# Operand formation, accumulated weight loads and small transposes in the seven-product FFN of a two-layer decoder trunk

## Chip, cores and metric

The kernel runs on one core of a Trainium2 chip. The metric is the device time of one execution in microseconds (us); where several runs are shown, their median counts. Engines are named as in the profile: PE is TensorE, DVE VectorE, ACT ScalarE, POOL GpSimd, SP SyncE.

## The reference, cut to what is computed

Two decoder layers on x of 512 tokens by 1024, all in float32. Each layer is a half-step SwiGLU FFN, a token mixer (layer 0: block-sparse attention, layer 1: pooling) and a second half-step FFN, each followed by a residual LayerNorm:

```python
def swiglu(x, w_gu, w_down):
    g, u = jnp.split(x @ w_gu, 2, axis=-1)        # 1024 -> 2 x 2816
    return (jax.nn.silu(g) * u) @ w_down          # 2816 -> 1024

for i in range(2):
    x = layer_norm(ALPHA * x + 0.5 * swiglu(x, ffn_w_gu[i, 0], ffn_w_down[i, 0]), ...)
    x = layer_norm(ALPHA * x + mixer_i(x), ...)
    x = layer_norm(ALPHA * x + 0.5 * swiglu(x, ffn_w_gu[i, 1], ffn_w_down[i, 1]), ...)
```

## The kernel before

**Passes.** Six phases follow each other: pass 0 FFN, 1 attention, 2 and 3 FFN, 4 pooling, 5 FFN (line 1009). Every float32 operand is split into a high half, copied by ACT (line 100), and the rest, which DVE subtracts (line 101); a product of two operands is then three matmuls (`mm3`, lines 103 to 107): high by low, high by high, low by high. The low half of the stationary operand is so wanted last, by line 107.

**Seven products.** A 2 x 2 block product is made with seven products of blocks in place of eight. The operands are sums and differences of the blocks: for weights in `Quad` (lines 132 to 148), for hidden activations in `Seven.seven` (lines 334 to 353). A product is known by its number 1 to 7; the order is 1, 2, 6, 5, 7, 3, 4 (`LATER`).

**Pieces and units.** A piece is 512 KB of weights, loaded by SP into a slot (line 215). The piece `s1` holds a21 + a22 and `s3` holds a21 + a11: SP loads a21, and once that has landed POOL issues a second, accumulating DMA that adds the other quarter (line 217). A unit is what one product needs of the weights, split into two halves in two more slots (`prepare`, line 227). Product 2 takes a12; product 6 takes a sum that DVE makes in place, a11 + s1, and also forms a12 + a11 + s1 for product 3 (`sums`, line 143); product 5 takes s1. Pieces are loaded in the order of the list `pieces`; down weights and attention's V weights come in two quads at once, whose pieces `two_quads` (line 166) interleaves as a11, a11, a12, a12, s1, s1, s3, s3, a22, a22. Units are split up to five ahead of the product that PE has finished (`PARTS`; `retire`, line 260, calls `run_ahead`).

**An FFN pass.** Quads 0 to 10 of gate and up columns give 256 hidden features each. Features 0 to 2047 go through the down projection in two groups of seven products (`down_product`, line 648), the rest through a plain product at the end. The first down group is placed inside quad 7 (`MIDDLE`): its product 1 comes ahead of the quad's product 4, the others behind it. The first group's hidden blocks are complete after quad 3. Its operands are made step by step by the generator `operands`: each `next(operands)` goes to the next `yield`. Before, steps stand behind (6, 7), (7, 7) and (3, 7), where (i, jj) is product i of quad jj, and behind the first five down products, there after `retire(2)`; four stand in the last quad for the second group. Operand 6 is made from `u2`, which uses the one buffer `ca` that the gate sums of each quad use too (line 692). Hidden operands 1 and 2 take two buffers of nine, of which the pass's own x takes seven; operand 6 takes the buffer that operand 1 leaves, operand 5 that of operand 2.

**Order.** PE's instructions run in the order of the text. Those of the other engines are put in order at build time by a planner: it keeps dependencies, prefers what stands earlier in the text, and by its own estimate of times fills an engine's free time with later work that is ready. On the chip each engine then works through its list in order, and waits where an input is not there. `tc.issue_after(ins)` keeps the instructions of its block that run on the engine of `ins` behind `ins`.

**Small inputs.** Pass 0 loads LayerNorm rows, a scale and the bias table's inputs at (1, 2) (`small_loads`, line 542). At (1, 6) `columns` (line 275) transposes the rows on PE into bank 6, from which DVE copies them (line 278), and `bias_rows` (line 553) then runs two matmuls into the same bank.

Of the kernel before, what the change touches and what calls it, by code (L numbers as in the profile page):

```python
# [28 lines left out]
ALU = mybir.AluOpType  # L29
# [30 lines left out]
MIDDLE = 7  # L60
# [23 lines left out]
def trunk(ctx, tc, x_in, xt, rel_bias, ln_g, ln_b, w_gu, w_dq, w_down, w_v, a_in, a_out, b_in, b_group, b_scale, b_out, onehot, out):  # L84
    nc = tc.nc
# [9 lines left out]
    def bank(i, name):  # L95
        return ps.tile([P, 512], F32, tag=f"b{i}", name=name)
# [6 lines left out]
    def mm3(acc, sh, sl, mh, ml, first, last, shared=False):  # L103

        nc.tensor.matmul(acc, sh, ml, start=first, stop=False, skip_group_check=shared)  # L105
        nc.tensor.matmul(acc, sh, mh, start=False, stop=False, skip_group_check=shared)  # L106
        nc.tensor.matmul(acc, sl, mh, start=False, stop=last, skip_group_check=shared)  # L107
# [8 lines left out]
    pieces, units, loaded = [], [], []  # L116
# [35 lines left out]
    QUADS = range(1, FF // 256)  # L152
# [12 lines left out]

    def two_quads(w, i):
        both = [Quad(w[i + q]) for q in range(2)]
        pieces[-10:] = [q.pieces[k] for k in range(5) for q in both]
        return both

    def ffn_units(l, m):
# [16 lines left out]
    for hp in range(H // 2):  # L188
        for part in (0, 1):
            a_plain(a_in[0], part * D + hp * 256)  # L190
        if hp == 0:
            both = two_quads(w_v, 0)
# [53 lines left out]
    def run_ahead(most=99):  # L246
        load_ahead()
        while len(parts) < min(len(units), taken[0] + most, retired[0] + PARTS + max(0, free() - 2) // 2 + early[0] + sum(i >= retired[0] for i in guests)):
            prepare()
            load_ahead()  # L250

    def weights():
        taken[0] += 1
        while len(parts) < taken[0]:
            while not all(p in loaded for p in units[len(parts)][1]):
                load()
            prepare()
        return parts[taken[0] - 1]

    def retire(count=1):  # L260

        retired[0] += count
        run_ahead()
# [11 lines left out]
    def columns(small):  # L275
        ct = bank(6, "cols_t")
        nc.tensor.transpose(ct[:, 0:2 * NL + NK], small[0:2 * NL + NK, GW + H:], ident[0:2 * NL + NK, 0:2 * NL + NK])
        nc.vector.tensor_copy(cols, ct[:, 0:2 * NL + NK])
# [24 lines left out]
    class Seven(Plain):  # L303
# [30 lines left out]
        def seven(self, b11, b21, b12, b22, room):  # L334

            self.take(1, b11)
            yield
            self.take(2, b21)
            yield
            nc.vector.tensor_tensor(b11, b11, b12, op=ALU.subtract)  # L340
            u2 = room()
            nc.vector.scalar_tensor_tensor(u2, b11, -1.0, b22, op0=ALU.mult, op1=ALU.subtract)
            yield
            self.take(6, u2)
            yield
            self.take(5, b11)
            yield
            self.form(7, b12, b12, -1.0, b22, ALU.add)
            yield
            self.take(3, b22)  # L350
            yield
            self.form(4, b21, u2, -1.0, b21, ALU.subtract)
            yield
# [188 lines left out]
    def small_loads():  # L542
        small = wp.tile([P, GW + H + P], F32, tag="slot", bufs=SLOTS, name="small")
        gs = wp.tile([H, GW], F32, tag="slot", bufs=SLOTS, name="gs")
        rows = small[:, GW + H:]
        nc.gpsimd.dma_start(rows[0:NL, :], ln_g.rearrange("l i (k p) -> (l i k) p", p=P))
        nc.gpsimd.dma_start(rows[NL:2 * NL, :], ln_b.rearrange("l i (k p) -> (l i k) p", p=P))
        nc.gpsimd.dma_start(rows[2 * NL:2 * NL + NK, :], b_scale[0].rearrange("(k p) -> k p", p=P))
        nc.gpsimd.dma_start(small[0:BUCKETS, 0:GW], onehot)
        nc.gpsimd.dma_start(small[0:BUCKETS, GW:GW + H], rel_bias)  # L550
        return small, gs
# [13 lines left out]

    BANKS = {1: 0, 6: 0, 7: 0, 4: 0, 2: 1, 5: 2, 3: 2}

    def ffn(n, x, dest):  # L570
        with tc.tile_pool(name=f"ffn{n}", bufs=1) as fp:
# [18 lines left out]
            def keep(i, jj, acc, bufs):  # L590
                kept[i, jj] = fp.tile([P, 512], F32, tag=f"kept{BANKS[i]}", bufs=bufs, name=f"kept{n}_{jj}_{i}")
                nc.scalar.activation(kept[i, jj], acc, AF.Copy)  # L592
# [43 lines left out]
            hid = [Seven(f"h{n}_{g}") for g in range(BLOCK // GROUP)]  # L636
# [11 lines left out]
            def down_product(i, g):  # L648


                if i in (1, 2, 5):
                    b0 = {1: (2, 6), 2: (0, 2), 5: (4, 4)}[i][g]
                    accs[g, BANKS[i]] = [bank(b0 + t, f"d{n}_{g}_{i}_{t}") for t in range(2)]
                acc = accs[g, BANKS[i]]
                for q in range(2):
                    wh, wl = weights()
                    for k in range(2):
                        c = slice(k * 512, (k + 1) * 512)
                        for t in range(2):
                            o = hid[g].parts[i][:, :, 2 * q + k, t * P:(t + 1) * P]  # L660
                            mm3(acc[t], o[:, 0], o[:, 1], wh[:, c], wl[:, c], q == 0 and k == 0 and i in (1, 2, 5),
                                q == 1 and k == 1 and i in (2, 3, 4), True)
                for t0, d, sign in {1: ((0, 0, 1),), 2: ((0, 0, 1),), 6: ((2, 0, 1),), 5: ((2, 1, -1),), 7: ((2, 1, -1),),
                                    3: ((2, 0, 1),), 4: ((0, 1, -1),)}[i]:
                    for t in range(2):
                        r = ax[:, t0 + t, d * 512:(d + 1) * 512]
                        nc.vector.scalar_tensor_tensor(r, acc[t], 0.5 / ALPHA * sign, r, op0=ALU.mult, op1=ALU.add)  # L667
                retire(2)
                if i in ((1, 2, 6, 5, 7) if g == 0 else (1, 2, 6, 5)):
                    next(operands)  # L670

            quads = {}
            for i, jj in ORDER:
                if jj >= FF:
                    down_product(i, jj - FF)
                    continue
                if n == 0 and (i, jj) == (1, 2):
                    with tc.issue_after(queued["acc"].ins):
                        onehots = small_loads()
                if n == 0 and (i, jj) == (1, 6):  # L680
                    columns(onehots[0])
                    bias_rows(*onehots)
                if n == 0 and i == 1 and 3 <= jj < 3 + NT:
                    with tc.issue_after(queued["load"].ins):
                        nc.sync.dma_start(ax[:, jj - 3, :], x_in[0, (jj - 3) * P:(jj - 2) * P, :])
                if (i, jj) == (1, 2):
                    load_residual()
                if i == 1:
                    quads[jj] = [bank(b, f"gu{n}_{jj}_{b}") for b in (2 * ((jj + 1) % 3), 2 * ((jj + 1) % 3) + 1)]
                if i == 2:  # L690
                    room(jj)
                    ca = fp.tile([P, 2, S], F32, tag="ca", name=f"ca{n}_{jj}")
                    cb = fp.tile([P, 2, 256], F32, tag="cb", name=f"cb{n}_{jj}")
                    quads[jj].append(bank(6 + jj % 2, f"gu{n}_{jj}_{6 + jj % 2}"))
                acc = quads[jj][BANKS[i]]
                for _ in product([acc[:, 0:256], acc[:, 256:512]], weights(), x.parts[i], i in (1, 2, 5), i in (2, 3, 4)):
                    pass
                if i in (1, 6):
                    keep(i, jj, acc, 2)
                elif i == 5:  # L700
                    keep(i, jj, acc, 1)
                elif i == 2:
                    add(ca[:, :, 0:256], acc, 1, jj)
                elif i == 3:
                    add(ca[:, :, 256:512], acc, 6, jj)
                    ins = gate(2 * jj, 0, 512, ca[:, 0, :], ca[:, 1, :], 1.0)
                    if 3 <= jj < 3 + NT:
                        update_residual(ins)
                elif i == 7:
                    add(cb, acc, 5, jj)  # L710
                    gate(2 * jj + 1, 256, 512, cb[:, 0, :], cb[:, 1, :], -1.0)
                else:
                    gate(2 * jj + 1, 0, 256, acc[:, 0:256], acc[:, 256:512], -1.0)
                retire()
                if jj == MIDDLE and i in (6, 7, 3) or jj == QUADS[-1] and i in (2, 6, 7, 3):
                    next(operands)

            pairs = {}
# [17 lines left out]
    def attention(n, x, dest):  # L736
        held[0] = 4
        with tc.tile_pool(name="att", bufs=1) as ap:
# [31 lines left out]
            def v_product(i):  # L770
                if i in (1, 2, 5):
                    accs[BANKS[i]] = [bank({1: 0, 2: 2, 5: 2}[i] + t, f"v{i}_{t}") for t in range(2)]
                acc = accs[BANKS[i]]
                for q in range(2):
# [285 lines left out]
```

## Time and profile before

| | |
|---|---|
| runs, us | 1695.34, 1691.97, 1692.09; median 1692.09 |
| profiled execution | 1694.32 us, of which span 1692.5 us |
| mean granted TensorE clock | 0.998 |
| PE busy | 1671.5 us, 99% |
| DVE busy | 1353.7 us, 80% |
| ACT busy | 865.8 us, 51% |
| POOL busy | 129.6 us, 8% |
| HBM read | 279.06 MB |

The span runs from the first to the last instruction of the profiled execution; the run's own time is 1.8 us longer. A busy share is an average over the whole span, and matmuls overlap, so the waits and the timelines of a stretch say more than the shares.

### The profile page before, as it was taken

The numbers are of one execution on the slowest core, as the hardware profiler recorded it, in microseconds if no ns is written. First come the engines' busy times: TensorE is split into PE (matmuls) and PEld (weight loads), VectorE is DVE, ScalarE is ACT, GpSimd is POOL, SyncE is SP. The second block draws the span as 40 slices with busy tenths as digits, with TensorE's granted clock in tenths as the row PEclk, the third lists the DMA queues.
The fourth block names the chain that finished last, engine by engine and source line by source line (L and its number), as shares of the span: only waits on it lengthen the run. The fifth ranks groups of instructions, "written<-read, shape, count | busy, mean of one in ns | idle before, by whom it ended". The sixth has DMA issues, their size and how long they took to land. (4 is left out here: it accounts for less than half of the span.)

```text
span 1692.5 us, 27752 instructions
## 1 busy us (share of the span) xinstructions
PE 1671.5 (99%) x11235; PEld 1547.8 (91%) x11235; DVE 1353.7 (80%) x1780; ACT 865.8 (51%) x1203; POOL 129.6 (8%) x172
## 2 busy tenths in 40 slices
PE   9999999999999999999999999999999999999998
PEld 9999899898888999979989999899898899998986
DVE  8686988798676878788788787897887887879697
ACT  6554555466444645545555555455454555445460
POOL 1102000000000001100000011000000101111000
PEclk9999999999999999999999999999999999999999
DMA  9778757805256177776683677866624647867541
GB/s 314 189 210 256 192 146 178 237 2 186 58 154 181 44 199 200 188 199 150 162 236 76 176 199 190 220 151 157 216 76 111 175 124 179 220 164 211 152 139 72
DMA packets 88848, 282.98 MB, mean 167 GB/s; under 512 B 8912, under 2 KB 22264, under 8 KB 88720
## 3 DMA queue, kind: packets, MB, share of 16 engines
q1 hardware_dynamic: 68304, 207.12, 36.9%
q0 software_dynamic: 20416, 74.09, 24.4%
q8 instruction: 88, 1.44, 0.3%
q14 instruction: 40, 0.33, 0.1%
HBM read 279.06 MB, written 4.74 MB: 168 GB/s over the span
## 5 line engine op out<-in xcount | busy, mean ns | idle before, releaser
L100 ACT ACTIVATE hi<-raw 128x1024 fp32r<-128x1024 f32 (+1 forms) x475 | 496.5, 1054 | 415.5 <-DVE lo L101 142.1
L101 DVE TENSOR_TENSOR lo<-raw,hi 128x1024 fp32r<-128x1024 f32 (+1 forms) x475 | 575.4, 1219 | 147.7 <-ACT hi L100 137.4
L105 PE MATMUL gu<-x,hi 128*128 128x256 f32 x2344 | 663.7, 283 | 1.6 <-DVE cb L595 0.9
L107 PE MATMUL gu<-x,lo 128*128 128x256 f32 x2344 | 663.6, 283 | 1.0 <-DVE lo L101 1.0
L106 PE MATMUL gu<-x,hi 128*128 128x256 f32 x2344 | 663.3, 283 | 0.0
L105 PEld LDWEIGHTS gu<-x,hi 128*128 128x128 f32 x2344 | 449.9, 192 | 3.7 <-DVE cb L595 1.3
L107 PEld LDWEIGHTS gu<-x,lo 128*128 128x128 f32 x2344 | 449.9, 192 | 1.6 <-DVE lo L101 1.6
L106 PEld LDWEIGHTS gu<-x,hi 128*128 128x128 f32 x2344 | 449.9, 192 | 0.4
L107 PE MATMUL d<-hi,xh 128*128 128x512 f32 x448 | 175.1, 391 | 7.1 <-DVE xh L101 7.1
L105 PE MATMUL d<-lo,xh 128*128 128x512 f32 x448 | 175.0, 391 | 0.2
L106 PE MATMUL d<-hi,xh 128*128 128x512 f32 x448 | 174.5, 389 | 0.0
L143 DVE TENSOR_TENSOR raw<-raw,raw 128x1024 f32<-128x1024 f32 x116 | 141.8, 1222 | 37.0 <-DMA raw<-in_ffn_w_dq 35.1
L217 POOL DMA_DIRECT2D raw<-in_ffn_w_gu x80 | 69.6, 870 | 797.3 <-DMA raw<-in_ffn_w_gu 325.2
L107 PEld LDWEIGHTS d<-hi,xh 128*128 128x128 f32 x448 | 84.1, 188 | 27.4 <-DVE xh L101 10.0
L105 PEld LDWEIGHTS d<-lo,xh 128*128 128x128 f32 x448 | 84.1, 188 | 18.1 <-DVE ca L595 0.6
L106 PEld LDWEIGHTS d<-hi,xh 128*128 128x128 f32 x448 | 84.1, 188 | 17.0
L592 ACT ACTIVATE kept<-gu 128x512 f32<-128x512 f32 x120 | 70.4, 587 | 48.4 <-PE gu L107 48.4
L105 PE MATMUL acc<-lo,h 128*128 128x512 f32 x192 | 75.2, 392 | 0.0
L107 PE MATMUL acc<-hi,h 128*128 128x512 f32 x192 | 74.7, 389 | 0.0
L106 PE MATMUL acc<-hi,h 128*128 128x512 f32 x192 | 74.7, 389 | 0.0
L101 DVE TENSOR_TENSOR x<-st,x 128x512 fp32r<-128x512 f32 (+1 forms) x65 | 56.0, 877 | 22.8 <-ACT x L100 22.5
L667 DVE SCALAR_TENSOR_TENSOR ax<-d,ax 128x512 f32<-128x512 f32 x112 | 72.5, 682 | 0.0
(176 smaller groups left out, 2234.6 us busy)
## 6 DMA issues: line engine op xcount, KB each, us to landing
raw<-in_ffn_w_gu SPq DMA_DIRECT2D x215, 512.0 KB, 4.9
raw<-in_ffn_w_gu POOLq DMA_DIRECT2D x80, 512.0 KB, 6.7
raw<-in_ffn_w_dq SPq DMA_DIRECT2D x80, 512.0 KB, 4.6
raw<-in_ffn_w_dq POOLq DMA_DIRECT2D x32, 512.0 KB, 7.7
raw<-in_ffn_w_down SPq DMA_DIRECT2D x24, 512.0 KB, 4.3
ax<-in_ln_b POOLq DMA_DIRECT2D x20, 512.0 KB, 8.0
raw<-in_a_w_in SPq DMA_DIRECT2D x16, 512.0 KB, 4.9
raw<-in_a_w_v SPq DMA_DIRECT2D x10, 512.0 KB, 4.5
```

The source lines that it names most:

```text
L100: nc.scalar.activation(hi, src, AF.Copy)
L101: return nc.vector.tensor_tensor(lo, src, hi.bitcast(F32), op=ALU.subtract)
L105: nc.tensor.matmul(acc, sh, ml, start=first, stop=False, skip_group_check=shared)
L106: nc.tensor.matmul(acc, sh, mh, start=False, stop=False, skip_group_check=shared)
L107: nc.tensor.matmul(acc, sl, mh, start=False, stop=last, skip_group_check=shared)
L143: nc.vector.tensor_tensor(d, d, more, op=ALU.add)
L217: queued["acc"] = nc.gpsimd.dma_start(p.tile, p.plus, accum_op=ALU.add)
L592: nc.scalar.activation(kept[i, jj], acc, AF.Copy)
L667: nc.vector.scalar_tensor_tensor(r, acc[t], 0.5 / ALPHA * sign, r, op0=ALU.mult, op1=ALU.add)
```

## The change

Five edits. (1) `two_quads` puts the s1 pieces in front of a12. (2) In `seven`, `b11 - b12` moves into the second step, and `b22 - b12`, until now formed with operand 7, gets a step of its own behind it; a group has nine steps instead of eight. (3) A list TAKES says behind which products a step is taken: four for the first group, at (6, 5), (6, 6), (3, 6) and (3, 7), and five in quad 10 for the second. (4) In `down_product` the step of an operand comes ahead of `retire(2)`, and in the first group's second product DVE's part of that `retire(2)` is held behind the operand just made. (5) `columns` moves from (1, 6) to (1, 4).

```diff
     def two_quads(w, i):
         both = [Quad(w[i + q]) for q in range(2)]
-        pieces[-10:] = [q.pieces[k] for k in range(5) for q in both]
+        pieces[-10:] = [q.pieces[k] for k in (0, 2, 1, 3, 4) for q in both]
...
             self.take(2, b21)
+            nc.vector.tensor_tensor(b11, b11, b12, op=ALU.subtract)
             yield
-            nc.vector.tensor_tensor(b11, b11, b12, op=ALU.subtract)
+            nc.vector.scalar_tensor_tensor(b12, b12, -1.0, b22, op0=ALU.mult, op1=ALU.add)
+            yield
             u2 = room()
...
-            self.form(7, b12, b12, -1.0, b22, ALU.add)
+            self.take(7, b12)
...
+    TAKES = [(6, 5), (6, 6), (3, 6), (3, MIDDLE)] + [(i, QUADS[-1]) for i in (2, 6, 7, 3, 3)]
...
-                retire(2)
                 if i in ((1, 2, 6, 5, 7) if g == 0 else (1, 2, 6, 5)):
                     next(operands)
+                with tc.issue_after(hid[g].last.ins) if g == 0 and i in (2,) else ExitStack():
+                    retire(2)
...
+                if n == 0 and (i, jj) == (1, 4):
+                    columns(onehots[0])
                 if n == 0 and (i, jj) == (1, 6):
-                    columns(onehots[0])
                     bias_rows(*onehots)
...
-                if jj == MIDDLE and i in (6, 7, 3) or jj == QUADS[-1] and i in (2, 6, 7, 3):
+                for _ in range(TAKES.count((i, jj))):
                     next(operands)
```

## Rows read from the trace of the kernel before

**Rows 1.** The page's head: the span, and of each engine the busy time, its share of the span and the instructions.

```profile
span 1692.5 us, 27752 instructions
PE 1671.5 (99%) x11235; PEld 1547.8 (91%) x11235; DVE 1353.7 (80%) x1780; ACT 865.8 (51%) x1203; POOL 129.6 (8%) x172
```

**Rows 2.** The waits of PE over the whole span: who waited for whom, us in total, times, longest us.

```profile
PE d L107 <- DVE xh L101: 7.1, 7, 1.6
...
PE gp L555 <- DVE cols L278: 0.9, 1, 0.9
PE gu L105 <- DVE cb L595: 0.9, 1, 0.9
```

**Rows 3.** The waits of PE in three stretches, the first down groups of passes 2 (720 to 760 us), 3 (1075 to 1115) and 5 (1515 to 1555), in this order.

```profile
PE d L107 <- DVE xh L101: 3.1, 2, 1.6
...
PE d L107 <- DVE xh L101: 2.0, 2, 1.5
...
PE d L107 <- DVE xh L101: 1.9, 2, 1.5
```

**Rows 4.** PE's timeline in the first down group of pass 2: start us, duration us, engine, line, operation, out<-in, shapes, count, and in brackets the idle time before it and what ended it.

```profile
738.57 0.39 PE L106 MATMUL d<-hi,xh 128*128 128x512 f32 x1
738.79 0.39 PE L107 MATMUL d<-hi,xh 128*128 128x512 f32 x1
...
741.38 0.50 PE L107 MATMUL d<-hi,xh 128*128 128x512 f32 x1 [1.58 <-DVE xh L101]
741.71 0.39 PE L105 MATMUL d<-lo,xh 128*128 128x512 f32 x1
```

**Rows 5.** DVE's timeline ahead of and in the first down group of pass 2, columns as above.

```profile
718.11 1.23 DVE L143 TENSOR_TENSOR raw<-raw,raw 128x1024 f32<-128x1024 f32 x1 [3.54 <-DMA raw<-in_ffn_w_dq]
...
725.21 1.23 DVE L143 TENSOR_TENSOR raw<-raw,raw 128x1024 f32<-128x1024 f32 x1 [4.74 <-DMA raw<-in_ffn_w_dq]
...
729.84 0.68 DVE L595 TENSOR_TENSOR cb<-gu,kept 128x512 f32<-128x512 f32 x1
...
736.64 1.22 DVE L342 SCALAR_TENSOR_TENSOR u<-hT 128x1024 f32<-128x1024 f32 x1
...
740.10 1.22 DVE L101 TENSOR_TENSOR xh<-u,xh 128x1024 fp32r<-128x1024 f32 x1
...
743.84 1.22 DVE L101 TENSOR_TENSOR lo<-raw,hi 128x1024 fp32r<-128x1024 f32 x1
...
746.18 1.22 DVE L101 TENSOR_TENSOR lo<-raw,hi 128x1024 fp32r<-128x1024 f32 x1
747.31 1.22 DVE L101 TENSOR_TENSOR xh<-hT,xh 128x1024 fp32r<-128x1024 f32 x1
```

**Rows 6.** The waits of DVE over the whole span, one row, columns as in rows 2.

```profile
DVE raw L143 <- DMA raw<-in_ffn_w_dq: 35.1, 15, 4.7
```

**Rows 7.** Busy time by stretch: from and to, length, then of each engine busy us and instructions, the granted clock, the DMA engines' busy share and GB/s. First the end of quad 7 ahead of the down group in pass 2, then the down group of pass 3, then the flight of one addition in pass 2.

```profile
709.60:729.60 20.00, 20.00 (x147) 18.82 (x145) 9.01 (x9) 7.29 (x9) 2.60 (x3) 1.00 0.98 226
...
1080.00:1120.00 40.00, 38.02 (x206) 32.57 (x205) 38.95 (x42) 23.04 (x25) 4.33 (x5) 1.00 0.79 213
...
777.86:783.60 5.74, 5.74 (x51) 5.74 (x50) 5.74 (x6) 2.81 (x4) 0.87 (x1) 1.00 0.59 94
```

**Rows 8.** The DMA issues of SP (two a12 loads, then two a21 loads) and of POOL (the first two additions) in pass 2, as timelines; then the DMA view's rows for single issues (KB, us from issue to landing): the additions issued at 707.70, 710.69 and, in quad 8, 777.86.

```profile
692.02 0.33 SPq L215 DMA_DIRECT2D raw<-in_ffn_w_dq  x1
...
697.77 0.33 SPq L215 DMA_DIRECT2D raw<-in_ffn_w_dq  x1
...
703.59 0.33 SPq L215 DMA_DIRECT2D raw<-in_ffn_w_dq  x1
...
706.41 0.33 SPq L215 DMA_DIRECT2D raw<-in_ffn_w_dq  x1
...
707.70 0.87 POOL L217 DMA_DIRECT2D raw<-in_ffn_w_dq  x1 [18.58 <-DMA raw<-in_ffn_w_dq]
...
710.69 0.87 POOL L217 DMA_DIRECT2D raw<-in_ffn_w_dq  x1 [1.22 <-ACT sg L599]
...
raw<-in_ffn_w_dq POOLq DMA_DIRECT2D x1, 512.0 KB, 10.3
...
raw<-in_ffn_w_dq POOLq DMA_DIRECT2D x1, 512.0 KB, 14.4
...
raw<-in_ffn_w_gu POOLq DMA_DIRECT2D x1, 512.0 KB, 5.7
```

**Rows 9.** DVE's timeline in quad 4 of pass 2: the two differences of the first group's blocks.

```profile
650.25 1.22 DVE L340 TENSOR_TENSOR hT<-hT 128x1024 f32<-128x1024 f32 x1
...
655.73 1.22 DVE L323 SCALAR_TENSOR_TENSOR hT<-hT 128x1024 f32<-128x1024 f32 x1
```

**Rows 10.** PE's timeline at (1, 6) of pass 0; then, of the instructions that touch the tile of small inputs, the last load (count, durations in ns, start of the first and last in us) and the us from issue to landing of its five loads.

```profile
129.47 0.25 PE L277 MATMUL cols_t<-ident,small 104*128 104x104 f32 x1
130.59 1.02 PE L555 MATMUL gp<-small 32*8 32x512 f32 x2 [0.87 <-DVE cols L278]
...
L550 POOL DMA_DIRECT2D small<-in_rel_bias x1: 498/498/498, 53.0 to 53.0; - x1
...
DMA to landing us min/median/max: 2.2/2.8/3.5
```

**Rows 11.** Attention's V products among PE's groups: line, engine, operation, out<-in, shapes, count, busy us, mean ns, idle us before them.

```profile
L107 PE MATMUL v<-hi,x 128*128 128x512 f32 x56 | 21.8, 390 | 0.0
```

## The prediction

> **What bounds the kernel now.** I read the page first: TensorE (PE) is busy 1671.5 of 1692.5 us [rows 1], so a change can give back at most the 21 us in which it stood still, unless it removes matmuls; this one removes none. Which waits these are is in the waits of PE. The largest is the third matmul of a product, which needs the low half of a hidden operand (`xh`, line 101): 7.1 us in 7 waits. One wait each belongs to the rows of the bias table (`gp`, 0.9 us) and to VectorE's (DVE's) sum `cb` (0.9 us) [rows 2]. The same view by stretches puts 3.1 us of the 7.1 into pass 2, 2.0 into pass 3 and 1.9 into pass 5, two waits each [rows 3]: always the first down group, its second and third products (operands 6 and 5). The remaining 0.1 to 0.2 us is pass 0.
>
> A wait costs more than its idle time. Matmuls of 512 columns start 0.22 us apart (738.57, 738.79), yet each is shown busy for 0.39, so a gap counted from that end hides 0.16; and after the wait the next start comes 0.33 later (741.38, 741.71), not 0.22 [rows 4]. Together a wait costs its gap plus about 0.27 us.
>
> Why is DVE late there? Its timeline in pass 2 shows it standing still for 3.54 us and again for 4.74, each time in front of a sum of down weights (line 143) that waits for a DMA; the sum `cb` that PE waits for, and `u`, from which operand 6 is split, queue behind [rows 5]. Over the whole run such sums wait 35.1 us [rows 6]. While it waits, DVE is busy 9.0 of 20 us, and in the down group that follows 38.95 of 40 [rows 7]: the idle time comes just before the stretch that has no room to make it up.
>
> The wait is for the accumulated quarters. In pass 2 SP issues the two a12 loads at 692.02 and 697.77 and the two a21 loads behind them at 703.59 and 706.41; POOL adds a22 onto these at 707.70 and 710.69, once they have landed, and the additions take 10.3 and 14.4 us [rows 8]. So they land at 718.0 and 725.1, and there DVE goes on (718.11, 725.21) [rows 5].
>
> **The change part by part.**
>
> *Order of the pieces.* The a21 loads take the issue times of the a12 loads. From load to addition the rows show 4.1 and 4.3 us (703.59 to 707.70, 706.41 to 710.69), so the additions would start at about 696 and 702. They land between 5.7 us later (an addition with little else in flight [rows 8]) and 14.4: the first at 702 to 711, the second at 708 to 716, against 718 and 725 now. The DVE places are about 714.6 (718.11 less its wait of 3.54) and, without that wait, 717. Both are met even at the slow end, so I take the 8.3 us of DVE waiting in pass 2 as gone, likewise in passes 3 and 5. What is late next: the a12 loads, now at 703.59 and 706.41, land by about 711; they feed the second product's units, which PE reaches only after it has waited for `cb`, past 729.84. On POOL the two additions pass the residual addition of line 447, which waits for a DVE product; it is needed only in the next LayerNorm, so I cost it at nothing, and 1 us at most were that cover gone. With DVE 8 us earlier, `cb` at 729.84 is on time: 0.9 + 0.27 = 1.2 us back. `u` at 736.64 waits only for the release of the buffer that it shares with the gate sums, and moves forward with them; operand 6, split at 740.10, is wanted at about 739.6 (741.38 less 1.58 and 0.16). Its waits, one in each of passes 2, 3 and 5, go.
>
> The rule that speaks against this move is in the Trainium skill, SBUF — State Buffer, "Who interferes with whom": DVE and GpSimd share a port pair, and a DVE instruction with two SBUF inputs, as nearly all here are, holds up a GpSimd instruction that reads SBUF. By it additions moved in among busy DVE would land later; the last rival says what that would give. The trace does not show it: an addition issued at 777.86, with DVE busy throughout (5.74 of 5.74 us), took 5.7 us, and the slowest, 14.4 us, had DVE idle for most of its flight [rows 7, 8].
>
> *Operands before weights.* `next(operands)` now stands ahead of `retire(2)`, and in the first group's second product the DVE halves of the new weights are held behind operand 5's. Today three weight halves, two of them at 743.84 and 746.18, run between operand 6 at 740.10 and operand 5 at 747.31 [rows 5], 1.14 us each. Operand 5 can move forward by up to 3.4 us, and the wait that it caused was 1.5 (the longest of passes 3 and 5 [rows 3]). So these waits go too, twice over. The price: three halves later by one operand, 1.14 us, units which PE reaches two products later. Cost 0, unless DVE idles at the barrier (third rival).
>
> *Differences amid the quads.* The text moves `b11 - b12` and `b22 - b12` up, but the planner has long put them there: in pass 2 lines 340 and 323 run at 650.25 and 655.73, 75 us before the down group [rows 9]. Worth 0; between a loss and a gain of 2 x 1.14 us per pass on DVE, which in the quads has room. The extra step in TAKES hands out the same instructions.
>
> *Columns apart.* The transpose of the small rows (129.47) and the bias matmuls (130.59) stand side by side, with a wait of 0.87 for the copy between them [rows 10]. Two quads apart, the copy is long done: 0.9 us back. The small rows are issued at the start of quad 2, by 53.0, and land within 3.5 us [rows 10]; the old place is quad 6, at 129.5, so the new one, quad 4, lies near 90, long after the landing. Issues on POOL stay as they are.
>
> *Attention's V weights* are loaded in the new order as well; their matmuls waited 0.0 us [rows 11], and their loads run far ahead. Cost 0, at most one wait of 1.6, the longest seen.
>
> **Sum.** Operands 6 and 5: 7.1 + 7 x 0.27 = 9.0. `cb` 1.2, columns 0.9. Together 11.1 us. The profiled execution took 1694.3 (span 1692.5), which leaves 1683.2. It lies 2.2 above the median of the runs, 1692.1. If those 2.2 are longer waits of the same kind, the end stays 1683.2; if they are a constant, it is 1681.0. One new wait of 1.6 somewhere adds as much: 1681.0 to 1684.8. I take the middle, **1683.0**.
>
> **Rivals.**
>
> 1. *Half of it.* The planner, which now believes the additions earlier, also places the sums earlier, and DVE again waits, for half as long as now. Then (9.0 + 1.2)/2 + 0.9 = 6.0 come back: 1686 to 1688.3. For: today's places were too early for the landings by 3.5 and 4.7 us. Against: earlier places lie in quads where DVE has room. Chance 0.14, nearly all of it faster.
>
> 2. *The wait changes its load.* The second product's units now wait for a12, 8.6 to 11.6 us later than before, DVE is as late as ever, and only the columns are won: 1691.2 to 1693.4. Against: PE wants those units 20 us after they land. Chance 0.08, no change.
>
> 3. *DVE stands at operand 5.* Its high half is copied into a buffer that the second product frees at its end, near 738 in pass 2. A DVE 8 us earlier reaches the fixed place of the low half before that and idles with weights queued behind it. All that now runs between the two operands takes 6.1 us (740.10 and 1.14 of its own, to 747.31 [rows 5]). If that idling reached PE whole in the four first groups, it would cost 24.4 against 11.1 won: 1705.4 on the median; half of it 1693.2. It turns the sign once more than 2.8 us per group get through. For: DVE is 97% busy there [rows 7]. Against: two sums leave the stretch, which frees 2.3 us, and weights are split five units ahead. Chance 0.07, slower.
>
> 4. *Additions held up by DVE*, as by the page's rule: they land where they land now, nothing but the columns is won, 1691.2 to 1693.4. Chance 0.03.
>
> **How the numbers follow.** The forecast has 0.68. About 0.2% (3.4 us) is what a measurement of this kernel tells from no change, so faster is below 1688.7. Faster: 0.68 + 0.12 of the first rival = 0.80. Same: the rest of the first, the second and the fourth = 0.13. Slower: 0.07. The range runs from 1679.4 (1681.0 less one unlisted wait of 1.6) to 1690.0, which takes in the first rival and leaves out the others, 0.18.
>
> **What would show it.** Right: line 143's waits for down weights fall from 35 us to under 10; `xh`, `cb` and `gp` leave the waits of PE; lines 340 and 323 stay where they are; PE's busy time is unchanged. Wrong: `xh` waits of PE that last; DVE waiting for ACT in front of operand 5; a wait of PE for `lo` in the first down group; sums that still wait for additions, with POOL's issues earlier.

## The result, and the profile after

The changed kernel takes 1681.4 us (median of 4 runs, 1680.9 to 1682.1) where the kernel before, beside it, takes 1692.6: ratio 0.9932, 95% interval 0.992 to 0.9944. The forecast was 1683.0, the range 1679.4 to 1690.0. Profile against profile it is 1682.12 against 1694.32, 12.2 us less; the sum had said 11.1.

The head of the page, to be read against [rows 1]:

```profile
span 1680.4 us, 27725 instructions
...
PE 1668.4 (99%) x11235; PEld 1548.7 (92%) x11235; DVE 1358.2 (81%) x1780; ACT 869.4 (52%) x1203; POOL 129.2 (8%) x172
```

PE's idle time fell from 21.0 to 12.0 us (span less busy), and its busy time by 3.1: the latter is not work, since the matmuls are as many, but the part of each wait that the matmul records, longer than the spacing of the starts, hide. Together 12.1, the difference of the spans.

PE runs the same matmuls in the same order in both kernels, the transpose of the columns aside, so the start of each can be set beside its start before. That tells where the time came back: 4.9 us in the first down group of pass 2 (with the end of quad 7 ahead of it), 2.6 and 2.5 in those of passes 3 and 5, 0.5 in that of pass 0, 1.0 at the bias matmuls, and 0.8 around the second groups of passes 2 and 3.

All waits of PE over the span, against [rows 2] (who, for whom: us in total, times, longest us):

```profile
PE idle L1006 <- DVE ax L1004: 1.1, 1, 1.1
PE gu L107 <- DVE lo L101: 1.0, 3, 0.6
PE gu L105 <- ACT hi L100: 0.6, 1, 0.6
PE o L105 <- DVE pr L819: 0.4, 1, 0.4
PE pt L831 <- DVE pr L823: 0.3, 1, 0.3
```

The waits for `xh`, `cb` and the columns are gone; what is left is the start of the program and attention. The DMA wait of line 143 [rows 6] no longer stands among DVE's waits at all.

The issues in pass 2, against [rows 8]: SP's two a21 loads now come first, then the two a12 loads; the last two lines are POOL's first two additions, which start before the a12 loads do.

```profile
690.77 0.33 SPq L215 DMA_DIRECT2D raw<-in_ffn_w_dq  x1
...
696.52 0.33 SPq L215 DMA_DIRECT2D raw<-in_ffn_w_dq  x1
...
702.35 0.33 SPq L215 DMA_DIRECT2D raw<-in_ffn_w_dq  x1
...
705.16 0.33 SPq L215 DMA_DIRECT2D raw<-in_ffn_w_dq  x1
...
696.87 0.86 POOL L217 DMA_DIRECT2D raw<-in_ffn_w_dq  x1 [9.00 <-DVE lo L101]
701.00 0.88 POOL L217 DMA_DIRECT2D raw<-in_ffn_w_dq  x1 [3.27 <-DVE raw L143]
```

The DMA view's row for the first of these (the second's reads the same): KB, us from issue to landing.

```profile
raw<-in_ffn_w_dq POOLq DMA_DIRECT2D x1, 512.0 KB, 7.7
```

The additions land at 704.6 and 708.7. DVE's timeline in the same place, against [rows 5] (start, duration, what, and in brackets the idle time before it):

```profile
713.24 1.22 DVE L143 TENSOR_TENSOR raw<-raw,raw 128x1024 f32<-128x1024 f32 x1
714.37 1.22 DVE L101 TENSOR_TENSOR lo<-raw,hi 128x1024 fp32r<-128x1024 f32 x1
715.62 1.23 DVE L143 TENSOR_TENSOR raw<-raw,raw 128x1024 f32<-128x1024 f32 x1
...
721.25 0.68 DVE L599 TENSOR_TENSOR cb<-gu,kept 128x512 f32<-128x512 f32 x1
...
728.05 1.22 DVE L344 SCALAR_TENSOR_TENSOR u<-hT 128x1024 f32<-128x1024 f32 x1
...
730.45 1.23 DVE L101 TENSOR_TENSOR xh<-u,xh 128x1024 fp32r<-128x1024 f32 x1
...
736.17 1.37 DVE L671 SCALAR_TENSOR_TENSOR ax<-d,ax 128x512 f32<-128x512 f32 x2 [0.76 <-PE d L107]
737.95 1.23 DVE L101 TENSOR_TENSOR xh<-hT,xh 128x1024 fp32r<-128x1024 f32 x1 [0.40 <-ACT xh L100]
```

The first two sums run at 713.24 and 715.62 without a wait; the data had been there for 7 to 9 us. Everything behind them is some 8 to 10 us earlier, of which 1.2 had been gained before this place: `cb` 721.25 instead of 729.84, `u` 728.05 instead of 736.64. In the down group DVE now even waits a little for PE and ACT, 0.76 and 0.40 us: it is ahead. By stretches (columns as in [rows 7]), the end of quad 7 in pass 2 and the down group of pass 3:

```profile
708.40:728.40 20.00, 20.00 (x147) 19.04 (x147) 16.37 (x18) 9.75 (x13) 1.73 (x2) 1.00 0.79 186
1070.00:1110.00 40.00, 40.00 (x214) 34.67 (x213) 38.11 (x40) 22.20 (x23) 4.32 (x5) 1.00 0.75 211
```

DVE is busy 16.4 of 20 us where it had been 9.0, and PE does not pause in the 40 us of the down group although DVE is 95% busy there.

### The profile page after: what moved, and what is told of

It reads as the page before. It is cut to its first block, busy times and chain, and to the rows that moved or that the text cites. A ratio compares the mean times of both kernels' runs of the same rounds, so it can differ in the third digit from the quotient of the medians.

```text
span 1680.4 us, 27725 instructions
## 1 busy us (share of the span) xinstructions
PE 1668.4 (99%) x11235; PEld 1548.7 (92%) x11235; DVE 1358.2 (81%) x1780; ACT 869.4 (52%) x1203; POOL 129.2 (8%) x172
## 3 DMA queue, kind: packets, MB, share of 16 engines
HBM read 279.06 MB, written 4.74 MB: 169 GB/s over the span
## 4 chain that ended last, share of the span: by engine, by line
PE 98%; DVE 1%; DMA 0%; ACT 0%; issue 0%; SPq 0%; DVEq 0%; ACTq 0%
PE gu L107 18%; PE gu L105 18%; PE gu L106 18%; PE d L105 6%; PE d L106 6%; PE d L107 6%; PE acc L105 4%; PE acc L107 4%; PE acc L106 4%; PE qk L106 2%; PE qk L107 2%; PE qk L105 2%; PE tp L373 1%; PE u L105 1%; PE u L107 1%; PE u L106 1%
```

## The experiments

Each run is set against the kernel before, run beside it: median 1692.57 us in the first four, 1692.83 in the last four. Theory A says that DVE's wait for the accumulated quarters is the cause of all; theory B, that operand 5 is late because halves of weights stand ahead of it on DVE; theory C, that the operand order and the columns add to A.

**1. The order of the pieces alone.**

```diff
-        pieces[-10:] = [q.pieces[k] for k in range(5) for q in both]
+        pieces[-10:] = [q.pieces[k] for k in (0, 2, 1, 3, 4) for q in both]
```

> The kernel before with one edit: the s1 pieces of the down and V quads are loaded in front of a12. Theory A (VectorE's wait for the accumulated quarters is the cause of all): that wait, 35 us before, falls under 2 us, the waits of TensorE for xh and cb all go, those for the columns stay: 9.5 to 10.5 us less than before, about 1682.4. Theory B (operand 5 is late because the weights' halves stand ahead of it on VectorE, whatever the loads do): cb and operand 6 come in time, the four waits for operand 5 stay (0.15 + 3 x 1.47 and 4 x 0.27 = 5.6 us), so only 4 to 5 us less, about 1688. Rival 1 of the prediction (sums planned earlier wait again): 5 to 6 us less, with DMA waits of line 143 left.

Measured: 1682.31 us, ratio 0.9942 (0.9929 to 0.9954), 10.3 us less. Of PE's waits only the columns' is left of those that the change removes:

```profile
PE idle L1000 <- DVE ax L998: 1.1, 1, 1.1
PE gp L555 <- DVE cols L278: 0.9, 1, 0.9
PE gu L107 <- DVE lo L101: 0.6, 1, 0.6
PE o L105 <- DVE pr L813: 0.5, 1, 0.5
PE pt L825 <- DVE pr L817: 0.3, 1, 0.3
```

Theory A holds. The planner put DVE's and ACT's instructions in the very same order as before, operation by operation, and PE's is the same as well, so nothing but the arrival of the data can have moved them; rival 1, by which the sums would be planned earlier, has no footing.

**2. Operands before weights alone.**

```diff
-                retire(2)
                 if i in ((1, 2, 6, 5, 7) if g == 0 else (1, 2, 6, 5)):
                     next(operands)
+                with tc.issue_after(hid[g].last.ins) if g == 0 and i in (2,) else ExitStack():
+                    retire(2)
```

> The kernel before with one edit: the operand's step ahead of retire(2), with the barrier in the first group's second product. Theory A: line 143 still waits some 35 us for down weights and cb's wait stays; operand 5 moves up by 3.4 us, which is more than it was late, operand 6 by 1.1 of the 0.4 to 1.6 us that it was late: 6 to 8 us less than before, about 1685. Theory B: as much as the whole change without the columns, 10 us less, about 1682.5. Rival 3 (VectorE stands at operand 5 with weights behind it): a wait of TensorE for lo in the first down group, and no gain or a loss.

Measured: 1691.19 us, ratio 0.999 (0.9982 to 0.9999), 1.4 us less: a fifth of what theory A had expected here. The largest of PE's waits:

```profile
PE d L107 <- DVE xh L101: 4.9, 8, 1.1
```

Of DVE's waits:

```profile
DVE raw L143 <- DMA raw<-in_ffn_w_dq: 34.1, 15, 5.5
```

PE's timeline in pass 2, in the products of operands 5 and 7:

```profile
744.35 0.50 PE L107 MATMUL d<-hi,xh 128*128 128x512 f32 x1 [0.33 <-DVE xh L101]
...
751.22 0.50 PE L107 MATMUL d<-hi,xh 128*128 128x512 f32 x1 [1.14 <-DVE xh L101]
```

DVE still waits for the additions, and the lateness has only moved down its list: operand 5's wait fell from about 1.5 to 0.33, but operand 7, which had been in time, is now 1.14 us late, and so in passes 3 and 5. Eight waits instead of seven. Neither theory had that; theory B is refuted by it, and A's sum for this edit was wrong. The wait for `cb`, which A had expected to stay, is not there either.

**3. The columns alone.**

```diff
+                if n == 0 and (i, jj) == (1, 4):
+                    columns(onehots[0])
                 if n == 0 and (i, jj) == (1, 6):
-                    columns(onehots[0])
```

> The kernel before with one edit: columns at (1, 4). All theories: the wait of TensorE for the copy of the columns goes and nothing else changes: 0.9 to 1.1 us less than before, about 1691.5. If the change of places disturbs the planner's order elsewhere: any other wait that moves.

Measured: 1692.45 us, ratio 1.0 (0.9991 to 1.0009). In its profile the wait for the columns is gone and the waits for `xh` are 7.4 us in 6; a gain of 0.9 is below what these runs can resolve, since the kernel before alone spreads from 1690.4 to 1697.0 over 27 runs. The starts of the matmuls show it all the same: behind the bias matmuls PE is 1.0 us earlier against the kernel before, in this run as in the changed kernel.

**4. The differences and TAKES alone** (in `seven` and at the quads, as in the diff of the change).

> The kernel before with one edit: the two differences earlier in the text and the steps behind the products of TAKES. Theory A: no change (within 0.5 us), since the planner already ran both differences in quad 4 and its lists for all engines come out the same. Rival: if the place in the text mattered, up to 2 x 1.14 us of VectorE's time per pass would leave the down group, and the wait for operand 5 would shorten by 1 to 2 us in each of passes 2, 3 and 5: 3 to 5 us less.

Measured: 1693.85 us, ratio 1.0005 (0.9996 to 1.0014): no change. The planner's order on DVE, ACT, SP and POOL is the same as before in every position. In the changed kernel too the two differences of pass 2 stand where [rows 9] had them, the 1.2 us earlier that all of this stretch is:

```profile
649.00 1.23 DVE L339 TENSOR_TENSOR hT<-hT 128x1024 f32<-128x1024 f32 x1
...
654.48 1.22 DVE L341 SCALAR_TENSOR_TENSOR hT<-hT 128x1024 f32<-128x1024 f32 x1
```

**5. All but the order of the pieces.**

```diff
-        pieces[-10:] = [q.pieces[k] for k in (0, 2, 1, 3, 4) for q in both]
+        pieces[-10:] = [q.pieces[k] for k in range(5) for q in both]
```

> The changed kernel with the pieces in the old order (a12 in front of s1). Theory A (the load order alone carries the gain): the waits of line 143 are back at 34 us, TensorE again waits for xh, now also for operand 7 as in the run with the operands first: about 1690.5, 1.5 to 2.5 us less than before and 9 more than the changed kernel. Theory C (operand order and columns add to it): 1688 or less.

Measured: 1689.72 us, ratio 0.9982 (0.9974 to 0.9991), 3.1 less than before and 8.3 more than the changed kernel. The wait of line 143 is back:

```profile
DVE raw L143 <- DMA raw<-in_ffn_w_dq: 31.6, 16, 4.3
```

and with it PE's waits for `xh`:

```profile
PE d L107 <- DVE xh L101: 4.0, 5, 1.1
```

The time lies between A's (1.5 to 2.5 less) and C's (1688 or less), nearer to A's: a little more is left to the other edits than A gave them. DVE's, ACT's and PE's orders are those of the changed kernel in every position, so the 8.3 us between the two come from the order of the pieces alone.

**6. The s1 pieces still later**, behind s3.

```diff
-        pieces[-10:] = [q.pieces[k] for k in range(5) for q in both]
+        pieces[-10:] = [q.pieces[k] for k in (0, 1, 3, 2, 4) for q in both]
```

> The kernel before with the s1 pieces loaded still later, behind s3. Theory A: in pass 2 the two additions land some 9 us later (the loads go from 703.59 and 706.41 to about 708 and 710, where they take 10 to 12 us to land, and the additions 8 to 10 more), VectorE waits that much longer in the quad, TensorE waits for cb in each first group: 10 to 30 us more than before. If VectorE's wait for the additions were not the cause: within 3 us of before.

Measured: 1757.49 us, ratio 1.0374 (1.0361 to 1.0388), 64.7 more. The direction is A's, the size more than twice its upper end. The three largest of PE's waits:

```profile
PE gu L105 <- DVE cb L595: 22.5, 8, 4.5
PE d L105 <- DVE lo L101: 18.4, 7, 3.4
PE d L107 <- DVE xh L101: 10.8, 8, 1.6
```

Of DVE's waits:

```profile
DVE raw L143 <- DMA raw<-in_ffn_w_dq: 83.9, 14, 12.7
```

DVE's timeline at the first sum of pass 2:

```profile
743.56 1.23 DVE L143 TENSOR_TENSOR raw<-raw,raw 128x1024 f32<-128x1024 f32 x1 [12.53 <-DMA raw<-in_ffn_w_dq]
```

PE's timeline behind one of its waits in pass 2:

```profile
745.98 0.50 PE L105 MATMUL d<-lo,xh 128*128 128x512 f32 x1 [2.50 <-DVE lo L101]
...
747.48 0.63 PE L107 MATMUL d<-hi,xh 128*128 128x512 f32 x1
747.90 0.63 PE L105 MATMUL d<-lo,xh 128*128 128x512 f32 x1
```

And the stretches ahead of and behind that wait, columns as in [rows 7]; the granted clock is the third number from the end:

```profile
741.00:745.90 4.90, 2.47 (x11) 1.69 (x9) 2.34 (x2) 0.00 (x0) 0.00 (x0) 1.00 0.91 210
747.00:750.40 3.40, 3.40 (x9) 2.32 (x7) 2.28 (x3) 1.95 (x2) 0.00 (x0) 0.50 0.00 0
```

The two waits of 3.54 and 4.74 in front of the first two sums of pass 2 [rows 5] have become one of 12.53. Three things make the end later than the sum had it. First, A counted the first groups alone. Matmul by matmul against the kernel before, these lose 23.9 us, which lies inside A's 10 to 30; the other 40.8 are lost around the second groups, where DVE had waited 11.3 us for additions in the kernel before and PE's list had shown no wait. Second, the halves of the weights queue behind the sums as well, and PE waits 18.4 us for them at the starts of products. Third, after a wait of 2.50 us the granted clock is 0.50, 1.2 GHz, from 747.0 to 750.4: matmuls start 0.42 us apart instead of 0.22. There are ten such stretches in the run, 40.9 us together, so that some 20 us are lost in them (an estimate, from these two spacings). PE's busy time is 1692.7 us against 1671.5 for the same matmuls, and its idle time 63.5 against 21.0: 21.2 and 42.5 make up the 63.7 us between the spans. The planner's order on DVE differs here from that of before in places, so the run is no pure shift in time of one transfer.

**7. Pieces and columns**, the edits of 1 and 3 together.

> The kernel before with two edits: the order of the pieces and the columns at (1, 4). Theory A: the same time as the changed kernel, 1681.4, within 0.7 us; the operand order, the barrier and the moved differences add nothing. Theory C: 1 us or more above the changed kernel, with waits for xh left.

Measured: 1681.52 us, ratio 0.9932 (0.992 to 0.9944): the changed kernel's time, within 0.1 us, and 0.8 below the pieces alone (1682.31; the runs of the two overlap). Beside the new order, operand order, barrier and differences add nothing that can be measured. No version here beats the changed kernel; this one equals it with two of its five edits.

**8. The old order without the addition onto s1.**

```diff
         pieces[-10:] = [q.pieces[k] for k in range(5) for q in both]
+        for q in both:
+            q.s1.plus = None
```

> The kernel before, old order of all, with one thing left out: the addition of a22 onto s1 of the down and V quads, so these weights are a21 alone. Its SP order and VectorE's list stay as before. Theory A (the landing of the addition is what VectorE waits for, not the place of the load): the DMA waits of line 143 fall under 4 us and TensorE's waits for xh and cb go, about 1682.5 as with the new order. Rival (the load order as such, slots or a12's place, is what counts): the waits stay, 1690 or more.

Measured: 1682.79 us, ratio 0.9937 (0.9925 to 0.9949), 10.0 less. No DMA wait of line 143 is left, and PE waits neither for `xh` nor for `cb`; the wait for the columns is there:

```profile
PE gp L557 <- DVE cols L280: 0.9, 1, 0.9
```

The loads stand where they stood, DVE's list is the same; taking the second transfer away gives what bringing it forward gives, and matmul by matmul it gives it in the same places: 4.94, 2.57 and 2.48 us in the first groups of passes 2, 3 and 5, in this run as in run 1. So it is the landing of the addition that DVE waited for.

## Why the prediction was right, point by point

**The bound.** That PE's stalls hang on DVE, and DVE's on the additions, is shown from three sides: earlier additions (run 1), none (run 8), later ones (run 6). The 35.1 us of DVE waiting were worth some 10 to 11 us of PE. Of the 35.1, 20.0 lay ahead of the first groups of passes 2, 3 and 5, and there 10.0 came back; the other 15, in pass 0 and around the second groups, gave back only 1.2.

**Order of the pieces.** Right in every step: the a21 loads took the a12 loads' times (696.52 against 697.77), the additions started at 696.9 and 701.0 (about 696 and 702), landed at 704.6 and 708.7 (inside 702 to 711 and 708 to 716), ahead of the sums. The a12 loads, issued at 702.35 and 705.16 instead of 692.02 and 697.77, were waited for by nobody. The places of the two sums, 714.6 and 717, were right too: 713.24 and 715.62, with the 1.2 us gained before.

**Operands before weights.** This step failed. "So these waits go too, twice over" does not hold of this edit by itself: alone it gave 1.4 us, and beside the new order nothing. The error was to count how far operand 5 can move (3.4 us) and not who then stands behind it on a full engine: the price, named as 1.14 us on weights that have time, was paid by operand 7. The sum was not hurt, because the waits had been counted once and the order of the pieces removes them.

**Differences amid the quads.** Worth 0, as said, and for the reason given: the build's order is the same.

**Columns.** The wait of 0.87 us is gone; the transpose now stands at 89.5, where "near 90" was said. In the times it shows only as the 0.8 between runs 1 and 7, which is less than their spread; the starts of the matmuls put it at 1.0.

**Attention's V weights.** Cost 0, as said: PE's list of waits after the change has none for them.

**The sum.** Gaps were put at 8.9 us and were 9.0; what the longer records hide was put at about 2.2 and was 3.1. By place, the first groups were put at 10.2 and gave 10.4, so the rule of gap plus 0.27 us holds to a few tenths; the columns were put at 0.9 and gave 1.0; the 0.8 around the second groups was in no term, since the list of waits shows none there. The sign "PE's busy time is unchanged" did not come true, and could not beside the prediction's own rule, by which part of each wait stands inside PE's busy time.

The forecast of 1683.0 was 1.6 too high. Median against median the change gave 11.2 us, the sum's 11.1 to a tenth. So the median came out nearer to 1681.0, the reading by which the 2.2 us between profile and median are a constant, than to 1683.2, the reading by which they are longer waits. The profiles speak for the second all the same: the profiled execution of the changed kernel lies only 0.7 above its median, so most of the excess went with the waits. Its 1683.2 is 1.8 too high because the sum was 1.1 short and 0.7 of the excess stayed. With one profile of each kernel that split is likely, not shown; by it, that 1681.0 came so near is in part luck, two errors that cancel.

**The rivals.** The first falls with run 1. The second does not occur: neither PE nor ACT waits for an a12 load. The third has its beginning: DVE waits 0.40 us for ACT in front of operand 5, which the prediction had named as a sign of being wrong, and 0.76 for PE just before. But that is 1.2 us in pass 2, where 2.8 per group would have turned the sign, and no wait of PE follows. The fourth falls too, and with it the prediction's step that an accumulating transfer issued by POOL is held up by busy DVE: the additions of the changed kernel flew while DVE was busy 5.87 of 7.70 and 6.45 of 7.75 us and took 7.7 us,

```profile
696.87:704.57 7.70, 7.70 (x66) 7.70 (x66) 5.87 (x7) 4.61 (x6) 1.74 (x2) 1.00 0.82 167
701.00:708.75 7.75, 7.75 (x67) 7.75 (x66) 6.45 (x8) 4.24 (x6) 1.74 (x2) 1.00 1.00 256
```

less than the 10.3 and 14.4 us of before beside an idler DVE. What was different then is the number of transfers in flight: 3.6 and 3.7 others on the mean while the two additions of before flew, 1.2 and 2.2 while those of the changed kernel did. Over all 116 additions of the kernel before, the time to landing grows with the number of others in flight (correlation 0.80) and not with DVE's busy share (-0.33); the changed kernel has 0.81 and -0.26. No run changes that number alone, so the cause stays likely, not shown.

## What to carry to other kernels

When the busiest engine is starved by a second one that is full, look upstream for where the second one stands idle: 8 us of waiting for a DMA just ahead of a full stretch cost more here than anything inside it. A transfer that goes in two steps (load, then add) wants to be issued earlier than one that goes in one; the reordering cost nothing here, because the overtaken load had slack. Moving one item forward in a full engine's list mostly chooses who is late (run 2). And a price for making something later has to count every place where the same transfer is used, as run 6 shows.

## What the runs showed of the hardware beyond that

Waits of 2.5 to 4.5 us on TensorE cost more than their length: in run 6 ten of them were each accompanied by a stretch at a granted clock of 0.50 (1.2 GHz instead of 2.4), and PE's busy time grew by 21.2 us; two others, of 2.60 and 2.73, were not. In the kernels before and after no wait inside the program was longer than 1.6 us, and the granted clock stayed at 1.00, 2.4 GHz, from 4 us to 1687 us before and from 5 to 1674 after.

An accumulating addition of 512 KB took between 5.0 and 14.4 us from issue to landing in the traces of these ten kernels, with medians of 6.6 to 7.2.

Kernels in which DVE waits for such additions mostly vary more from run to run: the standard deviation is 1.6 us over 27 runs before and 1.9 over 12 of run 5, against 0.8 in each of runs 1, 7 and 8, of five executions each. Run 2 is an exception, with 34.1 us of such waits and 0.8 over 11 executions, so that the waits are the reason is not shown.
